# A two-layer hybrid decoder trunk on one core: indexer scores by row halves, unnormalised differential softmaxes, longer booking of chained VectorE steps, and padded products

## The chip, the cores and the metric

The kernel runs on one core of a Trainium2 chip. The metric is the device time of one execution in microseconds (us), as a median over runs. Below, PE is the matrix engine (TensorE), PEld its loading of weights, DVE the VectorE, ACT the ScalarE, POOL the GpSimd, SP the engine that issues most DMAs.

## What is computed

Two layers over 256 tokens of width 1024, in float32. Each layer has a mixer of three attention groups (A, B, C) and a gated MLP, each followed by a layer norm:

```
h = LN(ALPHA*h + mixer(h));  h = LN(ALPHA*h + conv_gated_mlp(h))
A: s = q.k*scale + cum[q] - cum[k], causal;            o_a = softmax(s) v
B: score = sum_i w_i * relu(qi_i . ki) over 8 heads of 64, causal
   sel   = top 64 keys by score;                       o_b = softmax(q.k over sel) v
C: p0, p1 = two softmaxes of q.k over 64 columns each, causal
   o_c = rms_norm((p0 - lam*p1) v, g) * (1 - lam_init)
mixer = (g_a*(o_a W_a) + g_b*(o_b W_b) + g_c*(o_c W_c)) W_out
```

## The kernel before

**Weights.** All large products are made of two float32r halves: a weight tile of 128 x 512 is split into a high half (ACT copies it rounded) and a low half (DVE subtracts it from the raw tile); both stand in one tile `hl` (16 buffers, `HL_BUFS`). A product of activations and weights is then three matmuls, high-high, low-high, high-low (`mm3`, L397; `unit_x`, L652; `unit_w`, L679). One `hl` tile of 512 columns serves both blocks of 128 tokens, so it feeds six matmuls. Weights stream from HBM by SP in the order of use (`Stream`, L112).

**The order of the work.** The program is written out by Python generators. The main line emits the big projections; attention groups are side tasks that are advanced by `tick()` after each group of three matmuls. Where a task's next step is emitted is decided by a planner, `Clocks` (L196): it books an estimated cost for each instruction on its engine (`cost`, L205; `note`, L230), and `ready` (L387) holds a task back until the planner's clock says that its inputs are done. `refill` (L177) emits the next weight split by the same clocks. The engines themselves run their instructions in the order in which they were emitted. Every operation is issued in a wrapper (`Engine`, L259), so that all of them carry L267 in the profile, and the tile names tell them apart.

**The parts that the change touches**, once per layer each:
- `task_g1` (L722) makes, among other things, `augL` (16 x 256) and `augR` (16 x 4 x 256) on DVE: the cumulative forget gates of A as operands with 16 rows. `task_A` (L992) multiplies them into each of its three score banks, between the mask (`m`, `negid`, bf16) and the products of q and k.
- `task_index` (L859) computes the indexer: 8 heads of 64 rows, of which even heads lie in rows 0 to 63 of the operands and odd ones in rows 64 to 127. `jobs` are (query block, heads) in pairs, even heads and then odd ones, run by `par` side by side. Each job is one bank of scores, a relu on ACT, and a chain of DVE steps `s = rl * w + s`. Eight rounds of max and match-replace follow for the top 64, and then `sel`.
- `soften` (L900) is a softmax: negated row maximum (DVE), exponentials with row sums (ACT), reciprocal (DVE), and, with `norm`, a multiplication by it (DVE).
- `task_C` (L1006) makes two softmaxes, `a` (normalised) and `p` (not), combines them on DVE as `a = p * rinv + a`, where `rinv` holds -lam over the sum, transposes `a` on PE, multiplies by the values, and applies an RMS norm: squares on ACT with sums `ssq`, a power on POOL (`rr`), and a scaled copy on DVE (`oc`).

Rotary embedding (`rope`, L694) of the indexer's and of C's queries and keys is four DVE steps, after which PE transposes them (`task_rope_T`, L835). Banks of PSUM are taken by `att` (one) and `att2` (two at once).

Of the kernel before, what the change touches and what calls it, by code (L numbers as in the profile page):

```python
# [10 lines left out]
F32 = mybir.dt.float32  # L11
R32 = mybir.dt.float32r
# [183 lines left out]
class Clocks:  # L196
# [3 lines left out]
    def __init__(self):  # L200
        self.clk = dict(PE=0.0, DVE=0.0, ACT=0.0, POOL=0.0)
        self.done, self.by, self.read = {}, {}, {}
        self.table = "exp"

    def cost(self, eng, op, out, args):  # L205
        n = math.prod(out.shape[1:])
# [23 lines left out]
    def note(self, eng, op, args, kw):  # L230
        aps = [x for x in list(args) + list(kw.values()) if isinstance(x, bass.AP)]
        if op == "preload_act_table_set":
            self.clk[eng] += 1280
            self.table = "exp"
        if not aps:
            return
        out = aps[0]
        outs = [part(out)] + ([kw["accum_out"].name] if "accum_out" in kw else [])
        if op == "dma_start":
            self.done[out.name] = max(self.clk[eng], self.clk["PE"]) + 4000  # L240
            return
        start = max([self.clk[eng]] + [self.done.get(n, 0) for n in map(part, aps[1:]) if self.by.get(n) != eng])
        self.clk[eng] = start + self.cost(eng, op, out, aps)
        if "accum_out" in kw:
            self.clk[eng] += 155
        if eng == "ACT" and len(args) > 2 and args[2] in TABLES and TABLES[args[2]] != self.table:
            self.table = TABLES[args[2]]
            self.clk[eng] += 1280
        for o in outs:
            self.done[o] = self.clk[eng] + (150 if eng == "PE" else 230)  # L250
            self.by[o] = eng
        for x in aps[1:]:
            self.read[x.name] = self.clk[eng]
# [62 lines left out]
def tile_hybrid(ctx: ExitStack, tc: tile.TileContext, a: dict, out: bass.AP):  # L316
# [55 lines left out]
    def t4(shape, dt=F32, n="t4"):  # L372
        return s4.tile(shape, dt, name=nm(n), tag="s4")
# [7 lines left out]
    def t1(shape, n, dt=F32):  # L381
        return s1.tile(shape, dt, name=nm(n), tag="s1")
# [326 lines left out]
    def layer(l, hT, hflag):  # L709
# [12 lines left out]
        def task_g1(g1):  # L722
# [69 lines left out]
            chr_ = t1([16, 256], "chr", R32)  # L792
            cl = t1([16, 256], "cl")
            t_ = t1([16, 256], "ct")
            augL = t1([16, 256], "augL", R32)
            augR = t4([16, 4, 256], R32, "augR")
            col = lambda i: cst[0:16, C_COL + i:C_COL + i + 1]
            ve.tensor_copy(chr_, c16)
            ve.tensor_copy(ch, chr_.bitcast(F32))
# [5 lines left out]
            ve.scalar_tensor_tensor(ch, cl, col(5), ch, ALU.mult, ALU.add)  # L805
            for q in range(4):
                ve.tensor_scalar(augR[:, q, :], ch, cst[0:16, C_BM + q:C_BM + q + 1], None, ALU.mult)
            F["aug"] = (augL, augR)

            yield from ready("PE", kvT, wul)  # L810
            bk = yield from att()
# [47 lines left out]
        def task_index():  # L859
            yield from need("qiT", "kiT", "biw")  # L860
            qiT, kiT, biw = F["qiT"], F["kiT"], F["biw"]
            s0 = t2([P, P], n="s0")
            s1 = t2([P, 256], n="s1")
            sx = [s0, s1]

            jobs = [(0, [0, 2, 4, 6]), (0, [1, 3, 5, 7]), (1, [0, 2]), (1, [1, 3]), (1, [4, 6]), (1, [5, 7])]

            def job(qb, hs):
                kw = P * (qb + 1)
                bk = yield from att()  # L870
                for n, i in enumerate(hs):
                    o = 64 * (i % 2)
                    mm(bk[:, n * kw:(n + 1) * kw], qiT[o:o + 64, i // 2, qb * P:(qb + 1) * P],
                       kiT[o:o + 64, 0:kw], n == 0)
                yield from ready("ACT", bk)
                rl = t2([P, len(hs), kw])
                sc.activation(rl, bk.rearrange("p (n k) -> p n k", n=len(hs)), AF.Relu)
                att_free(bk)
                for n, i in enumerate(hs):
                    prev = (m38[:, 256 - kw:256] if i == 0 else sx[qb])  # L880
                    ve.scalar_tensor_tensor(sx[qb], rl[:, n, :], biw[:, qb, i:i + 1], prev, ALU.mult, ALU.add)

            for i in range(0, 6, 2):
                yield from par(job(*jobs[i]), job(*jobs[i + 1]))
            mx = small([P, 2, 8], "mx")
            for r in range(TOPK // 8):
                yield from ready("DVE", s0, s1)
                for qb in (0, 1):
                    ve.max(mx[:, qb, :], sx[qb])
                for qb in (0, 1):  # L890
                    ve.match_replace(sx[qb], mx[:, qb, :], sx[qb], PICKED)
                yield
            sb0 = cpool.tile([P, P], BF16, name=nm("sb0"), tag="sb0")
            sb1 = cpool.tile([P, 256], BF16, name=nm("sb1"), tag="sb1")
            ve.scalar_tensor_tensor(sb0, s0, PICK_T, m01[:, P:256], ALU.is_gt, ALU.add)
            ve.scalar_tensor_tensor(sb1, s1, PICK_T, m01, ALU.is_gt, ALU.add)
            F["sel"] = (sb0, sb1)


        def soften(bk, ms, pt, rinv, norm=True):  # L900

            yield from ready("DVE", bk)
            v = bk.rearrange("p (n k) -> p n k", n=len(ms))
            mx = small([P, 4], "smx")
            ve.tensor_reduce(mx[:, :len(ms)], v, AX.X, ALU.max, negate=True)
            sm = small([P, 4], "ssm")
            for n, m in enumerate(ms):
                sc.activation(pt[:, m, :], v[:, n, :], AF.Exp, bias=mx[:, n:n + 1],
                              accum_out=sm[:, n:n + 1])
# [96 lines left out]
        def task_C():  # L1006
# [2 lines left out]
            a0, p0 = t2([P, 4, P], n="a0"), t2([P, 4, P], n="p0")  # L1009
            a1, p1 = t4([P, 4, 256], n="a1"), t4([P, 4, 256], n="p1")  # L1010
            rina = small([P, 2, 4], "rina")
            rinv = small([P, 2, 4], "rinv")

            def scores(qb, ms):
# [5 lines left out]
                for n, m in enumerate(ms):  # L1020
                    for c in range(2):
                        mm(bks[c][:, n * kw:(n + 1) * kw],
                           qcT[64 * c:64 * c + 64, m, qb * P:(qb + 1) * P],
                           kcT[64 * c:64 * c + 64, m, 0:kw], False)
                yield from par(soften(bks[0], ms, (a0, a1)[qb], rina[:, qb, :]),
                               soften(bks[1], ms, (p0, p1)[qb], rinv[:, qb, :], norm=False))
            yield from par(scores(0, [0, 1, 2, 3]), scores(1, [0, 1]), scores(1, [2, 3]))
            ve.tensor_scalar(rinv, rinv, nlam[:, l:l + 1], None, ALU.mult)
            for qb, (pp, aa) in enumerate(((p0, a0), (p1, a1))):
                for m in range(4):  # L1030
                    ve.scalar_tensor_tensor(aa[:, m, :], pp[:, m, :], rinv[:, qb, m:m + 1], aa[:, m, :],
                                            ALU.mult, ALU.add)
            yield from ready("PE", a0, a1)
            q0 = t4([P, 4, 256], n="q0")
            q1 = t2([P, 4, P], n="q1")
# [6 lines left out]
            def job(qb):  # L1042
# [6 lines left out]
                yield from ready("ACT", bk)  # L1049
                for m in range(4):  # L1050
                    sc.activation(oc[:, qb, m * P:(m + 1) * P], bk[:, m * P:(m + 1) * P], AF.Square,
                                  accum_out=ssq[:, qb, m:m + 1])
                ve.tensor_scalar(ssq[:, qb, :], ssq[:, qb, :], 1.0 / P, RMS_EPS, ALU.mult, ALU.add)
                gp.tensor_tensor(rr[:, qb, :], ssq[:, qb, :], mhalf[:, :4], ALU.pow)
                yield from ready("DVE", rr)
                for m in range(4):
                    ve.scalar_tensor_tensor(oc[:, qb, m * P:(m + 1) * P], bk[:, m * P:(m + 1) * P],
                                            rr[:, qb, m:m + 1], dg[:, l, :], ALU.mult, ALU.mult)
# [340 lines left out]
```

## Time and profile before

| | |
|---|---|
| median of 3 runs | 927.51 us (927.25 to 927.71) |
| the profiled execution | 927.42 us |
| its span, first to last instruction | 925.6 us |
| PE busy | 903.9 us, 98% |
| DVE busy | 658.6 us, 71% |
| ACT busy | 510.4 us, 55% |
| POOL busy | 46.4 us, 5% |
| mean share of the granted PE clock | 0.996 |

Shares of busy time are averages over the span. In the timeline, each line gives the start, the duration of the run of equal instructions, and in brackets the idle time before it with what ended it. Matmuls overlap in the record: what one costs is the distance from its start to the next start. A float32 matmul stands as two.

### The profile page before, as it was taken

The numbers are of one execution on the slowest core, as the hardware profiler recorded it, in microseconds if no ns is written. First come the engines' busy times: TensorE is split into PE (matmuls) and PEld (weight loads), VectorE is DVE, ScalarE is ACT, GpSimd is POOL, SyncE is SP. The second block draws the span as 40 slices with busy tenths as digits, with TensorE's granted clock in tenths as the row PEclk, the third lists the DMA queues.
The fourth block names the chain that finished last, engine by engine and source line by source line (L and its number), as shares of the span: only waits on it lengthen the run. The fifth ranks groups of instructions, "written<-read, shape, count | busy, mean of one in ns | idle before, by whom it ended". The sixth has DMA issues, their size and how long they took to land. (4 is left out here: it accounts for less than half of the span.)

```text
span 925.6 us, 14457 instructions
## 1 busy us (share of the span) xinstructions
PE 903.9 (98%) x5329; PEld 787.8 (85%) x5329; DVE 658.6 (71%) x1283; ACT 510.4 (55%) x1006; POOL 46.4 (5%) x63
## 2 busy tenths in 40 slices
PE   7999999999999999999999999999999999999996
PEld 4877887888888999999988788888888799999995
DVE  7788677766678766766787956667667886766755
ACT  4754765655537655655455455665555375655540
POOL 6100000011000000000000000000110100000000
PEclk9999999999999999999999999999999999999999
DMA  8823356556636665565444323548675385566501
GB/s 289 303 91 114 95 171 231 193 199 221 204 122 225 215 200 187 180 200 182 131 157 152 113 91 114 188 138 286 187 245 172 119 277 186 177 192 186 180 18 46
DMA packets 46681, 161.47 MB, mean 174 GB/s; under 512 B 5841, under 2 KB 6865, under 8 KB 46609
## 3 DMA queue, kind: packets, MB, share of 16 engines
q1 hardware_dynamic: 44208, 155.20, 51.1%
q0 software_dynamic: 1408, 4.98, 1.7%
q8 instruction: 42, 0.69, 0.3%
q10 hardware_dynamic: 992, 0.35, 0.1%
q14 instruction: 31, 0.25, 0.1%
HBM read 159.47 MB, written 1.05 MB: 173 GB/s over the span
## 5 line engine op out<-in xcount | busy, mean ns | idle before, releaser
L267 DVE TENSOR_TENSOR hl<-raw,hl 128x512 fp32r<-128x512 f32 (+1 forms) x578 | 387.3, 696 | 186.6 <-ACT hl L267 184.7
L267 ACT ACTIVATE hl<-raw 128x512 fp32r<-128x512 f32 (+1 forms) x584 | 347.4, 625 | 192.9 <-PE att L267 94.1
L267 PE MATMUL acc<-hl,hTh 128*128 128x512 f32 (+1 forms) x896 | 276.8, 390 | 2.5 <-ACT hTh L267 2.1
L267 PE MATMUL att<-hTh,hl 128*128 128x256 f32 x1280 | 231.5, 283 | 0.0
L267 PEld LDWEIGHTS att<-hTh,hl 128*128 128x128 f32 x1280 | 200.8, 192 | 1.4
L267 PEld LDWEIGHTS acc<-hl,hTh 128*128 128x128 f32 x896 | 166.9, 188 | 37.7 <-ACT hTh L267 3.7
L267 PE MATMUL att<-hTl,hl 128*128 128x256 f32 x640 | 181.1, 283 | 0.0
L267 PE MATMUL acc<-hl,hTl 128*128 128x512 f32 (+1 forms) x448 | 165.5, 387 | 0.9 <-DVE hTl L267 0.9
L267 PE MATMUL acc<-hl,act 128*128 128x512 f32 x528 | 123.4, 390 | 0.0
L267 PEld LDWEIGHTS att<-hTl,hl 128*128 128x128 f32 x640 | 122.8, 192 | 0.0
L267 PEld LDWEIGHTS acc<-hl,act 128*128 128x128 f32 x528 | 97.9, 188 | 19.5
L267 PEld LDWEIGHTS acc<-hl,hTl 128*128 128x128 f32 x448 | 84.5, 189 | 17.7 <-DVE hTl L267 2.4
L267 PE MATMUL acc<-hl,oT 128*128 128x512 f32 x288 | 68.3, 391 | 0.0
L267 PEld LDWEIGHTS acc<-hl,oT 128*128 128x128 f32 x288 | 53.7, 188 | 10.9
L267 DVE SCALAR_TENSOR_TENSOR cv<-att,convp,cv 128x255 f32<-128x255 f32 x88 | 40.4, 480 | 16.1 <-ACT cv L267 14.5
L267 PE MATMUL acc<-hTh,hl 128*128 128x256 f32 x256 | 48.7, 289 | 3.0 <-DVE hl L267 2.6
L267 PE MATMUL acc<-hl,mT 128*128 128x512 f32 x192 | 45.4, 392 | 0.0
L267 PEld LDWEIGHTS acc<-hTh,hl 128*128 128x128 f32 x256 | 39.9, 191 | 5.5 <-DVE hl L267 3.2
L267 PEld LDWEIGHTS acc<-hl,mT 128*128 128x128 f32 x192 | 35.6, 188 | 7.1
L267 ACT ACTIVATE hTh<-att 128x512 fp32r<-128x512 f32 x16 | 9.6, 597 | 49.1 <-PE att L267 43.1
L267 PE MATMUL acc<-hTl,hl 128*128 128x256 f32 x128 | 36.2, 283 | 0.0
L267 ACT ACTIVATE t<-att 128x512 f32<-128x512 f32 (+1 forms) x32 | 18.2, 599 | 28.3 <-PE att L267 23.1
(162 smaller groups left out, 686.6 us busy)
## 6 DMA issues: line engine op xcount, KB each, us to landing
raw<-in_w_dram SPq DMA_DIRECT2D x284, 512.0 KB, 4.3
raw<-in_w_dram SPq DMA_DIRECT2D x8, 332.0 KB, 3.8
lng<-in_ln_g_dram POOLq DMA_DIRECT2D x4, 512.0 KB, 4.2
lnb<-in_ln_b_dram POOLq DMA_DIRECT2D x4, 512.0 KB, 5.5
h<-in_x_dram SPq DMA_DIRECT2D x4, 256.0 KB, 4.7
lng<-in_ln_in_g_dram SPq DMA_DIRECT2D x1, 512.0 KB, 8.1
lnb<-in_ln_in_b_dram SPq DMA_DIRECT2D x1, 512.0 KB, 10.2
wu<-in_w_ukv_dram POOLq DMA_DIRECT2D x2, 256.0 KB, 5.8
```

The costliest lines, as they stand in the source:

```text
L267: f(*args, **kw)
```

## The change

It has six parts. (1) The indexer's scores are emitted by one job for each of three (query block, heads) groups; it takes two banks at once and alternates matmuls of an even head (rows 0 to 63) with the next odd head's (rows 64 to 127). The groups run one after another. (2) `augL` and `augR` get 128 partitions, which POOL sets to zero; the sixteen rows are written as before, and A multiplies all 128. (3) C's first softmax is no longer normalised: the row sums `suma` are kept, `rinv` becomes -lam * suma / sum(p), so that `a` carries a factor `suma`, which `rina` takes out again at the squares (a scale on ACT) and in `rr` (one more small DVE step for each query block). (4) The combining steps are emitted in pairs, with a yield after each. (5) The planner books 110 ns more for a DVE instruction that reads what the DVE instruction before it wrote. (6) By that, most of the mixer's order comes out differently.

```diff
-        self.table = "exp"
+        self.table, self.prev = "exp", ""
...
         start = max([self.clk[eng]] + [...])
+        if eng == "DVE" and self.prev in map(part, aps[1:]):
+            start += 110
         self.clk[eng] = start + self.cost(eng, op, out, aps)
+        if eng == "DVE":
+            self.prev = part(out)
...
-            augL = t1([16, 256], "augL", R32)
-            augR = t4([16, 4, 256], R32, "augR")
+            augL_ = t1([P, 256], "augL", R32)
+            augR_ = t4([P, 4, 256], R32, "augR")
+            gp.memset(augL_.bitcast(F32), 0.0)
+            gp.memset(augR_.bitcast(F32), 0.0)
+            augL, augR = augL_[0:16], augR_[0:16]
...
-            F["aug"] = (augL, augR)
+            F["aug"] = (augL_, augR_)
...
-            jobs = [(0, [0, 2, 4, 6]), (0, [1, 3, 5, 7]), (1, [0, 2]), (1, [1, 3]), (1, [4, 6]), (1, [5, 7])]
             def job(qb, hs):
                 kw = P * (qb + 1)
-                bk = yield from att()
+                bks = yield from att2()
                 for n, i in enumerate(hs):
-                    o = 64 * (i % 2)
-                    mm(bk[:, n * kw:(n + 1) * kw], qiT[o:o + 64, i // 2, qb * P:(qb + 1) * P],
-                       kiT[o:o + 64, 0:kw], n == 0)
-                yield from ready("ACT", bk)
...
+                    for c in range(2):
+                        o = 64 * c
+                        mm(bks[c][:, n * kw:(n + 1) * kw], qiT[o:o + 64, i // 2, qb * P:(qb + 1) * P],
+                           kiT[o:o + 64, 0:kw], n == 0)
+                for c, bk in enumerate(bks):
+                    yield from ready("ACT", bk)
...
+                    yield
...
-            for i in range(0, 6, 2):
-                yield from par(job(*jobs[i]), job(*jobs[i + 1]))
+            for qb, hs in ((0, [0, 2, 4, 6]), (1, [0, 2]), (1, [4, 6])):
+                yield from job(qb, hs)
...
-            sm = small([P, 4], "ssm")
+            sm = small([P, 4], "ssm") if sums is None else sums[:, ms[0]:]
...
-                yield from par(soften(bks[0], ms, (a0, a1)[qb], rina[:, qb, :]),
-                               soften(bks[1], ms, (p0, p1)[qb], rinv[:, qb, :], norm=False))
+                yield from par(soften(bks[0], ms, (a0, a1)[qb], rina[:, qb, :], False, suma[:, qb, :]),
+                               soften(bks[1], ms, (p0, p1)[qb], rinv[:, qb, :], False))
...
-            ve.tensor_scalar(rinv, rinv, nlam[:, l:l + 1], None, ALU.mult)
+            ve.scalar_tensor_tensor(rinv, rinv, nlam[:, l:l + 1], suma, ALU.mult, ALU.mult)
             for qb, (pp, aa) in enumerate(((p0, a0), (p1, a1))):
                 for m in range(4):
+                    if m % 2 == 0:
+                        yield from ready("DVE", pp)
                     ve.scalar_tensor_tensor(aa[:, m, :], pp[:, m, :], rinv[:, qb, m:m + 1], aa[:, m, :],
                                             ALU.mult, ALU.add)
+                    if m % 2:
+                        yield
...
                     sc.activation(oc[:, qb, m * P:(m + 1) * P], bk[:, m * P:(m + 1) * P], AF.Square,
-                                  accum_out=ssq[:, qb, m:m + 1])
+                                  scale=rina[:, qb, m:m + 1], accum_out=ssq[:, qb, m:m + 1])
...
                 yield from ready("DVE", rr)
+                ve.tensor_tensor(rr[:, qb, :], rr[:, qb, :], rina[:, qb, :], ALU.mult)
```

The order of the instructions moves in three places of which the prediction speaks. In the rows, a name's last number tells instances apart.

**PE, layer 0, where C's queries are transposed** (`ident` with the tile `t_89`; `hl` are weights, `sb` is `sel`, `kbT` and `t_22` the keys and queries of B). Before:

```order
L267 MATMUL acc_848<-hl_777,hTh_162 128x512
L267 MATMUL acc_848<-hl_777,hTl_163 128x512
L267 MATMUL acc_848<-hl_777,hTh_162 128x512
L267 MATMUL att_876<-ident,t_89_845 128x128 x4
L267 MATMUL att_881<-ident,t_89_845 128x128 x4
L267 MATMUL acc_849<-hl_777,hTh_162 128x512
```

In the changed order:

```order
L271 LDWEIGHTS negid
L271 MATMUL att_1035<-sb_95_991,negid 128x512
L271 MATMUL att_1035<-kbT_739,t_22_440 128x128 x4
L271 LDWEIGHTS negid
L271 MATMUL att_1041<-sb_96_992,negid 128x512
L271 MATMUL att_1041<-kbT_739,t_22_440 128x256 x2
L271 LDWEIGHTS negid
L271 MATMUL att_1045<-sb_96_992,negid 128x512
L271 MATMUL att_1045<-kbT_739,t_22_440 128x256 x2
L271 MATMUL att_1050<-ident,t_89_830 128x128 x4
L271 MATMUL acc_939<-hl_995,hTh_162 128x512
```

The transposes stood some 33 projection matmuls after the indexer's last scores; now they stand behind 102 of them and behind B's three banks of scores.

**DVE, layer 0, where C's two softmaxes are combined** (`a`, `p` and `rinv` as above, `hl` the low halves of weights, `q` and `oT` evacuations). Before:

```order
L267 TENSOR_TENSOR hl_1336<-raw_975,hl_1336 128x512
L267 RECIPROCAL rinv_1140<-ssm_1252 128x2
L267 TENSOR_SCALAR rinv_1140<-rinv_1140,nlam 128x8
L267 SCALAR_TENSOR_TENSOR a_122_1135<-p_123_1136,rinv_1140,a_122_1135 128x128 x4
L267 SCALAR_TENSOR_TENSOR a_124_1137<-p_125_1138,rinv_1140,a_124_1137 128x256 x4
L267 TENSOR_TENSOR hl_1363<-raw_1024,hl_1363 128x512
```

In the changed order:

```order
L271 RECIPROCAL rinv_1184<-ssm_1273 128x2
L271 SCALAR_TENSOR_TENSOR rinv_1184<-rinv_1184,nlam,suma_1183 128x8
L271 SCALAR_TENSOR_TENSOR a_122_1178<-p_123_1179,rinv_1184,a_122_1178 128x128 x2
L271 TENSOR_TENSOR hl_1415<-raw_1018,hl_1415 128x512
L271 COPY q_147_1398<-att_1405 128x4x128
L271 SCALAR_TENSOR_TENSOR a_122_1178<-p_123_1179,rinv_1184,a_122_1178 128x128 x2
L271 TENSOR_TENSOR hl_1437<-raw_1104,hl_1437 128x512
L271 SCALAR_TENSOR_TENSOR a_124_1180<-p_125_1181,rinv_1184,a_124_1180 128x256 x2
L271 TENSOR_TENSOR hl_1465<-raw_1104,hl_1465 128x512
L271 TENSOR_TENSOR oT_1454<-att_1455,oT_1454 128x512
L271 TENSOR_TENSOR oT_1454<-att_1460,oT_1454 128x512
L271 SCALAR_TENSOR_TENSOR a_124_1180<-p_125_1181,rinv_1184,a_124_1180 128x256 x2
```

The eight combining steps stood in one piece, with the splits of weights behind them; now a split follows every two or so. The multiplications of `a` by `rina` (four groups before this place) are gone.

**DVE, at the start of the program, between the first norm's two scalings and its second block's transposed values** (`h_92`, `h_93` the scaled rows, `att` banks with their transposes, `gb` gain and bias). Before:

```order
L267 TENSOR_SCALAR h_93<-h_93,mv_220,rs_223 128x512
L267 TENSOR_TENSOR hl_284<-raw_116,hl_284 128x332
L267 TENSOR_TENSOR hl_291<-raw_116,hl_291 128x332
L267 TENSOR_TENSOR att_297<-att_297,gb 128x512 x2
L267 TENSOR_TENSOR att_304<-att_304,gb 128x512 x2
L267 TENSOR_TENSOR hTl_163<-att_297,hTh_162 128x4x128
```

In the changed order:

```order
L271 TENSOR_SCALAR h_93<-h_93,mv_220,rs_223 128x512
L271 TENSOR_TENSOR hl_284<-raw_116,hl_284 128x332
L271 TENSOR_TENSOR hl_291<-raw_116,hl_291 128x332
L271 TENSOR_TENSOR hl_297<-raw_119,hl_297 128x332
L271 TENSOR_TENSOR att_301<-att_301,gb 128x512 x2
L271 TENSOR_TENSOR att_308<-att_308,gb 128x512 x2
L271 TENSOR_TENSOR hTl_163<-att_301,hTh_162 128x4x128
```

A third split of 332 columns, which stood behind the low halves `hTl`, now stands ahead of the four steps on the banks.

POOL has four more instructions: two memsets in each layer (128 x 256 and 128 x 1024), behind the second load of `lamq` in layer 0 and behind the power for `rr` of the latent's norm in layer 1, and ahead of C's powers. The queue of SP is unchanged.

## Rows read from the trace of the kernel before

**Rows 1.** The page's part 1: busy us, share of the span, instructions.
```profile
PE 903.9 (98%) x5329; PEld 787.8 (85%) x5329; DVE 658.6 (71%) x1283; ACT 510.4 (55%) x1006; POOL 46.4 (5%) x63
```

**Rows 2.** Waits of PE: tile waited for, us in total, times, longest.
```profile
PE att L267 <- DVE t L267: 3.4, 2, 1.8
PE acc L267 <- DVE hl L267: 2.6, 3, 1.4
...
PE acc L267 <- ACT hl L267: 0.5, 1, 0.5
```

**Rows 3.** Timeline of PE, three places: start, us, instruction, count, idle before.
```profile
20.74 1.78 PE L267 MATMUL acc<-hl,hTh 128*128 128x512 f32 x4 [1.44 <-ACT hTh L267]
...
72.11 0.74 PE L267 MATMUL att<-ident,t 128*128 128x128 f32 x5 [1.80 <-DVE t L267]
...
120.93 0.39 PE L267 MATMUL acc<-hTh,hl 128*128 128x256 f32 x1 [1.40 <-DVE hl L267]
```

**Rows 4.** Timeline of DVE, layer 0: indexer, first rounds, C's queries, combining steps.
```profile
59.21 2.74 DVE L267 SCALAR_TENSOR_TENSOR s<-t,biw,s 128x128 f32<-128x128 f32 x7
...
65.10 2.11 DVE L267 SCALAR_TENSOR_TENSOR s<-t,biw,s 128x256 f32<-128x256 f32 x4
...
69.51 0.61 DVE L267 MAX8 mx<-s 128x8 f32<-128x128 f32 x2
...
70.68 0.42 DVE L267 TENSOR_TENSOR ru<-t,cc 128x256 f32<-128x256 f32 x1
...
117.55 2.72 DVE L267 SCALAR_TENSOR_TENSOR a<-p,rinv,a 128x128 f32<-128x128 f32 x8
120.19 1.89 DVE L267 TENSOR_TENSOR hl<-raw,hl 128x512 fp32r<-128x512 f32 x3
```

**Rows 5.** Timeline of PE, layer 0, scores of A.
```profile
146.66 0.39 PE L267 MATMUL att<-m,negid 128*128 128x512 bf16 x1
146.98 0.50 PE L267 MATMUL att<-augR,augL 16*128 16x512 f32 x1
147.41 1.16 PE L267 MATMUL att<-t,t 128*128 128x128 f32 x8
148.41 0.27 PE L267 MATMUL att<-m,negid 128*128 128x256 bf16 x1
148.61 0.50 PE L267 MATMUL att<-augR,augL 16*128 16x512 f32 x1
149.03 1.13 PE L267 MATMUL att<-t,t 128*128 128x256 f32 x4
```

**Rows 6.** Timeline of PE, layer 0, scores of B behind a projection.
```profile
83.69 0.39 PE L267 MATMUL acc<-hl,hTh 128*128 128x512 f32 x1
83.92 0.39 PE L267 MATMUL att<-sb,negid 128*128 128x512 bf16 x1
84.15 1.05 PE L267 MATMUL att<-kbT,t 128*128 128x128 f32 x8
85.04 0.38 PE L267 MATMUL att<-sb,negid 128*128 128x512 bf16 x1
```

**Rows 7.** Timeline of PE, layer 0: the indexer's first scores and C's first scores.
```profile
56.94 1.71 PE L267 MATMUL att<-kiT,t 64*128 64x128 f32 x16
...
97.56 1.16 PE L267 MATMUL att<-t,t 64*128 64x128 f32 x16
```

**Rows 8.** The same view: the indexer's second scores, then C's.
```profile
59.48 1.14 PE L267 MATMUL att<-kiT,t 64*128 64x256 f32 x8
...
98.98 1.13 PE L267 MATMUL att<-t,t 64*128 64x256 f32 x8
```

**Rows 9.** Timeline of DVE at the start of the program.
```profile
17.75 0.90 DVE L267 TENSOR_TENSOR hl<-raw,hl 128x332 fp32r<-128x332 f32 x2
```

**Rows 10.** POOL's instructions by group: count, busy us, mean ns, idle before.
```profile
L267 POOL TENSOR_TENSOR mrg<-mrg,gs 128x1024 f32<-128x1024 f32 x4 | 11.0, 2752 | 171.5 <-DVE gs L267 171.5
```

**Rows 11.** Timeline of ACT, layer 0, one relu of the indexer.
```profile
62.07 0.60 ACT L267 ACTIVATE t<-att 128x512 f32<-128x512 f32 x1 [0.78 <-DVE s L267]
```

More of the change, by code (lines that the diff above doesn't have):

```diff
@@ L864, in task_index @@
             sx = [s0, s1]
-            jobs = [(0, [0, 2, 4, 6]), (0, [1, 3, 5, 7]), (1, [0, 2]), (1, [1, 3]), (1, [4, 6]), (1, [5, 7])]
             def job(qb, hs):
                 kw = P * (qb + 1)
-                bk = yield from att()
+                bks = yield from att2()
                 for n, i in enumerate(hs):
-                    o = 64 * (i % 2)
-                    mm(bk[:, n * kw:(n + 1) * kw], qiT[o:o + 64, i // 2, qb * P:(qb + 1) * P],
-                       kiT[o:o + 64, 0:kw], n == 0)
-                yield from ready("ACT", bk)
[L876 to L881, printed above, removed]
-            for i in range(0, 6, 2):
-                yield from par(job(*jobs[i]), job(*jobs[i + 1]))
+                    for c in range(2):
[4 more added lines that the diff above has]
+                    yield from ready("ACT", bk)
+                    rl = t2([P, len(hs), kw])
+                    sc.activation(rl, bk.rearrange("p (n k) -> p n k", n=len(hs)), AF.Relu)
+                    att_free(bk)
+                    for n, i in enumerate(hs):
+                        prev = (m38[:, 256 - kw:256] if i + c == 0 else sx[qb])
+                        ve.scalar_tensor_tensor(sx[qb], rl[:, n, :], biw[:, qb, i + c:i + c + 1], prev,
+                                                ALU.mult, ALU.add)
+                    yield
+            for qb, hs in ((0, [0, 2, 4, 6]), (1, [0, 2]), (1, [4, 6])):
+                yield from job(qb, hs)
             mx = small([P, 2, 8], "mx")
@@ L897, in task_index, with soften @@
             F["sel"] = (sb0, sb1)
-        def soften(bk, ms, pt, rinv, norm=True):
+        def soften(bk, ms, pt, rinv, norm=True, sums=None):
             yield from ready("DVE", bk)
@@ L1011, in task_C @@
             rina = small([P, 2, 4], "rina")
+            suma = small([P, 2, 4], "suma")
             rinv = small([P, 2, 4], "rinv")
```

## The prediction

> **What bounds the kernel now.** I read the busy shares first: PE is busy for 98% of the span, DVE for 71%, ACT for 55% [rows 1]. So the time is the length of PE's list plus the pauses in it, and DVE or ACT count only where PE stops for them. The waits of PE come next [rows 2]. Of those that this change can reach, two, 3.4 us in all, are transposes that wait for a rotated tile of DVE; three, 2.6 us, are projections that wait for a low half of weights from DVE, and one, 0.5 us, for a high half from ACT. The timeline gives them their places [rows 3]: C's query transposes at 72.11 after 1.80 us (the twin in layer 1 has the other 1.6), a projection at 120.93 after 1.40, and the first product of the program at 20.74 after 1.44 for `hTh`. Last, what DVE does before each of them [rows 4]. Before 72.11 it runs the indexer's chained steps `s` (seven in 2.74 us, 0.39 each; four wide ones in 2.11, 0.53 each), one top-k round (69.51 to 70.68, 1.17 us) and the rotation. `cost` books a step at 110 + 1.2 ns a column, 264 and 417 ns. Eight steps of each are 8 x 0.125 + 8 x 0.11 = 1.9 us more than booked: about the wait. Before 120.93 it runs eight combining steps without a break, 117.55 to 120.19, and the split that PE needs stands behind them.
>
> The sum is made against the profiled execution, 927.42 us, 0.1 under the median; about 1.8 us of it lie outside its span of 925.6.
>
> **The waits, -6.5 us.** With 110 ns more per chained step, the planner books 374 and 527 ns, what the rows show. It now puts C's query transposes behind 102 projection matmuls and B's banks. On DVE, the rotation stands behind the last round, `sel` and three splits. It is done near 89.0 (the sum is below) and PE is there near 90.2: the two waits for `t` go, -3.4. The eight combining steps are parted, a split behind each two, so a split waits for two steps (0.7 us) instead of eight (2.6), and DVE loses the four multiplications by `rina` ahead of them: -2.6. I also count the 0.5 of ACT's high half as gone, as it stands next to the same places. The low end of this term is nothing at all; see the first rival.
>
> **Padded products, -2.3 us.** In A's first bank the mask's product takes 0.32 to the next start, the one of 16 rows 0.43, and the products of q and k 1.00: 1.75 us [rows 5]. B's bank is the same but for the 16 rows and shows the price when every product has 128: 0.23 for a mask product behind a 128-row one, 0.89 for the eight [rows 6]. The 16-row product is 256 columns in two records, and with 128 rows I take it at 0.23, as a projection of 512 columns [rows 6]. That makes 0.23 + 0.23 + 0.89 = 1.35, a gain of 0.40. A wide bank now has 0.20 for the mask and 0.42 for the 16 rows [rows 5]; I take 0.12 (half the columns of the 0.23) and 0.23, and 0.11 off the first product behind, as above: 0.38. Per layer 0.40 + 2 x 0.38 = 1.16. Bounds: nothing, if a product of 16 rows costs its 0.43 for another reason; not more than the 0.43 + 0.32 - 0.23 = 0.52 of the first bank three times over, 3.1 in two layers.
>
> The Trainium skill ("TensorE: Matmul & The Clock Gate", "Why this matters for your kernels") says that a single matmul with 32 rows takes the same time as one with 128, rows being saved by running tiles beside each other only. By it alone this term would be 0 and the time 920.5; that is the third rival. The skill's page "TensorEngine Tiling (Array Packing)" (on changing the tiling mode) has PE drained at the change, which the 0.32 and 0.43 beside 0.23 agree with, and which the padding avoids.
>
> The zeroing is on POOL, which is idle here. Four memsets: the nearest row, a product of 128 x 1024, is 2752 ns [rows 10], which I take as the upper end; the lower is next to nothing. They are issued before the sixteen rows are computed, so DVE's writes to `augL` and `augR` wait only if POOL comes late. I take 0; at worst, where a whole 2.75 us is in the way, DVE is some 1.5 us late in each layer at a place where PE has splits in store, +1 in all.
>
> **Alternating the indexer's halves, -1.1 us.** The first scores of query block 0 run for 1.71 us, sixteen records of one half after the other's; C's, of the same shape and already alternating, for 1.16 [rows 7]: -0.55 in each layer. The wide scores take 1.14 already, as C's alternating ones do (1.13) [rows 8]: nothing there.
>
> **The start, +0.4 us.** A third split of 332 columns stands ahead of DVE's four steps on the banks; two take 0.90 us [rows 9], one 0.4. The next wait there is PE's for `hTh` [rows 3], which comes from those banks, so 1.44 becomes about 1.85. Nothing hides it: PE has nothing else to do there. Lower bound 0 if the split's data come late enough that ACT sets the chain; upper 0.45.
>
> **The top-k of layer 0, +0.3 us.** The projections that were spread around C's transposes now run in one stretch that DVE must feed while it does the top-k. PE: first scores from 56.94, now done at 58.1; six matmuls, 1.5 (three took 0.83 between the first scores and the wide ones [rows 7, 8], and three more at 0.23); wide scores 1.1; six matmuls, 1.5; wide scores 1.1: at 63.4 the stretch begins, and 102 x 0.23 = 23.5 us later, at 86.9, come B's masks. DVE: first step at 59.21 - 0.55 = 58.7, then 16 steps (8 x 0.39 + 8 x 0.53 = 7.3), seven rounds before the last split (8.2), and 15 splits at 1.89 / 3 = 0.63 (9.5) [rows 4]. Split by split, in the order of the program, I set DVE's end beside PE's first use: the third comes at 67.9 and is used at 68.2, the fourth 69.7 and 69.6, the fifth (behind the second round) 71.5 and 71.0, the seventh 73.9 and 73.7, the last 83.7 and 84.8. So PE is short of a tile by up to 0.5 us in the first rounds, and not later. I take 0.3. Nothing is the lower bound; a DVE that begins 1.5 us later than I have it would make 2. Behind it the last round (1.17), `sel` (0.9, as one step `s` of each width), three splits (1.9) and the rotation (three times the 0.42 of its first step) end near 89.0; PE, after three banks of B at 85.04 - 83.92 = 1.12 [rows 6], is there at 90.2. In layer 1 the rotation still stands behind the first round and I find it 0.5 us ahead of PE: 0.
>
> **At nothing:** the scale on ACT's squares (an operand, no instruction); the two small steps on `rr`, each behind POOL's power and ahead of `oc`, for which PE has projections and the next group of scores; the `suma` factor (it replaces a step). If that cover were gone, two small steps in each layer, at most as long as a step of 128 columns (0.39), are 1.6. The queue of SP is unchanged.
>
> **Sum:** 927.42 - 6.5 - 2.3 - 1.1 + 0.4 + 0.3 = 918.2 us.
>
> **Rivals.**
> *The waits move instead of going.* DVE does nearly the same work, and where a stall of PE goes, PE asks for the next split earlier; a place after B's scores or behind the combining steps may be late next. For it: the top-k stretch has margins of 0.3 us and less, and POOL's and ACT's shares of C's chain are unchanged. Against it: DVE is idle for 29% of the span and sixteen tiles of `hl` can stand ready. Half of the 6.5 back gives 921.5, all of it 924.7. Chance 0.22.
> *Lock step of ACT and DVE in the indexer, slower.* A relu of ACT waits for DVE's steps on the tile whose place it takes; this is in the trace of before: 0.78 us ahead of a relu of 0.60 [rows 11]. The new job emits both relus of a pair in a row, with high halves behind them on ACT, and DVE's low halves wait for these. If relu and split followed each other strictly, each of the twelve relus of the program would cost PE, whose stretch has no cover, 0.60 + 0.63 = 1.23 us: 14.8 us, 933.0. It decides from the ninth of twelve on (9 x 1.23 = 11.1, over the gain of 9.2 and the 1.9 to be seen). Against it: even now that relu waits 0.78, and PE's list of waits has none for it. Chance 0.05.
> *Padding gives nothing:* what the skill's rule above says of a single product; by the rows, that the 0.43 belongs to the data type or to the shape of the output. 918.2 + 2.3 = 920.5. Against it the 0.32 ahead of the 16-row product, which a cost of its own can't explain. Chance 0.08.
> *All waits back and no gain of the padding:* 927.0, chance 0.03.
>
> **How the numbers follow.** The forecast has 0.62. The range runs from 916.0 (a padding of 3.1, no price at the start or in the top-k, 916.7, and 0.7 for smaller waits) to 923.0 (half of the waits back, and 1.5 from the memsets or DVE's late start). It leaves out the lock step, the combined case and the waits that come back whole, together a little under 2 in 10. A measurement of this kernel tells 0.2%, 1.9 us, from no change: faster is below 925.6, slower above 929.4. Faster are the forecast, the padding rival and most of the first: 0.90; the same 0.05; slower, the lock step, 0.05.
>
> **What will show it.** In the profile after: no line for DVE's `t` among PE's waits, and `hl` at 0.5 us or less; a start-to-start distance of 0.23 behind the padded product, and no longer first product of q and k; 1.1 us for the indexer's first scores; the wait at the first product near 1.85; waits of up to 0.5 in the 102 matmuls; POOL's memsets done before DVE writes `augL`. I am wrong if PE's waits on DVE add up to over 3 us again, if they reappear inside the top-k stretch, or if ACT's relus there wait longer than the 0.78 of before and PE with them.

## The result, and the profile after

| | before | changed |
|---|---|---|
| median | 927.61 us (4 runs, 927.25 to 927.90) | 917.07 us (4 runs, 916.76 to 917.12) |
| span of the profiled execution | 925.6 us | 915.0 us |
| ratio | | 0.9885, 95% interval 0.9871 to 0.9899 |

The forecast was 918.2 us in a range of 916.0 to 923.0, with 0.90 on faster. The time came out 1.1 us under it. How much of that is right for the reasons given is what the rest is about: some of the steps were wrong, and their errors partly cancel.

The page's part 1 of the changed kernel, to be set beside [rows 1]. PE's share is the same 98%; its busy time fell by 4.3 us, and the rest of the 10.6 us was idle time.

```profile
PE 899.6 (98%) x5329; PEld 787.5 (86%) x5329; DVE 654.2 (71%) x1271; ACT 510.7 (56%) x1006; POOL 49.3 (5%) x67
```

All waits of PE in the changed kernel (tile waited for, us in total, times, longest):

```profile
PE acc L271 <- ACT hTh L271: 4.0, 8, 2.1
PE att L271 <- DVE spin L271: 1.1, 1, 1.1
PE att L271 <- DVE h L271: 0.8, 1, 0.8
PE acc L271 <- DVE hl L271: 0.3, 1, 0.3
PE acc L271 <- POOL hl L271: 0.3, 1, 0.3
PE acc L271 <- ACT hl L271: 0.3, 1, 0.3
```

Against [rows 2], the line of DVE's `t` (3.4 us) is gone, `hl` of DVE fell from 2.6 to 0.3, and ACT's from 0.5 to 0.3. New is that `hTh` of ACT stands at 4.0 us with eight waits, where it was 2.1 with two. (The line of DVE's `h`, 0.8 us here, is at the start; it varies from one execution to the next, with 2.2 us for the same order in the kernel with 16 rows below.)

The timeline of PE in the changed kernel, at the start, the indexer, B's scores, behind C's first scores, A's scores, and a layer norm (start, us, instruction, count, idle before):

```profile
21.16 2.08 PE L271 MATMUL acc<-hl,hTh 128*128 128x512 f32 x4 [2.08 <-ACT hTh L271]
...
57.53 1.16 PE L271 MATMUL att<-kiT,t 64*128 64x128 f32 x16
...
87.25 0.39 PE L271 MATMUL att<-sb,negid 128*128 128x512 bf16 x1
...
90.52 0.60 PE L271 MATMUL att<-ident,t 128*128 128x128 f32 x4
...
110.93 0.39 PE L271 MATMUL acc<-hTh,hl 128*128 128x256 f32 x1 [0.28 <-ACT hl L271]
111.66 0.38 PE L271 MATMUL acc<-hTh,hl 128*128 128x256 f32 x1 [0.34 <-DVE hl L271]
...
143.53 0.39 PE L271 MATMUL att<-m,negid 128*128 128x512 bf16 x1
143.57 0.58 PE L271 MATMUL att<-augR,augL 128*128 128x512 f32 x1
143.99 1.05 PE L271 MATMUL att<-t,t 128*128 128x128 f32 x8
144.88 0.27 PE L271 MATMUL att<-m,negid 128*128 128x256 bf16 x1
...
272.06 1.20 PE L271 MATMUL acc<-hl,hTh 128*128 128x512 f32 x4 [0.25 <-ACT hTh L271]
```

- The indexer's first scores take 1.16 us, as C's did, instead of 1.71 [rows 7].
- A's narrow bank, from mask to mask, takes 144.88 - 143.53 = 1.35 us instead of 1.75 [rows 5], as forecast. Mask and product together take 143.99 - 143.53 = 0.46, the 0.23 + 0.23 of the sum (the record parts them as 0.04 and 0.42, so neither can be read by itself), and the products of q and k 0.89 instead of 1.00.
- B's masks come at 87.25 (forecast 86.9) and C's query transposes at 90.52 (90.2), without a wait. In the stretch of 102 matmuls ahead of them no wait is recorded.
- The first product waits 2.08 us for `hTh`, where 1.85 was forecast. It starts 0.42 us later than before (21.16 against 20.74 [rows 3]).

Both kernels run the same 4656 projection matmuls in the same order, so the start of the n-th one in both traces shows where the 10.6 us came from (a table of mine from the two traces; differences are taken before rounding):

| place | before | changed | difference | since the place above |
|---|---|---|---|---|
| start, projection 160 | 53.90 | 53.82 | -0.09 | -0.09 |
| end of A in layer 0, 560 | 157.52 | 152.52 | -5.00 | -4.91 |
| behind the first norm of layer 0, 1120 | 292.54 | 287.66 | -4.88 | +0.12 |
| behind the norm between the layers, 2400 | 482.82 | 478.32 | -4.50 | +0.38 |
| end of A in layer 1, 2880 | 606.97 | 596.20 | -10.78 | -6.28 |
| behind the first norm of layer 1, 3440 | 742.38 | 731.72 | -10.66 | +0.12 |
| near the end, 4640 | 913.45 | 902.79 | -10.65 | +0.01 |

So the two mixers gave 11.2 us, three norms took 0.6 back, and the start shows no difference between these two executions.

POOL's memsets in layer 0, which the sum had at nothing, took 0.33 and 0.97 us and were done over 8 us ahead of DVE's first write to `augL`, at 49.37 (in layer 1 over 8 us as well):

```profile
39.70 0.33 POOL L271 MEMSET augL<- 128x256 f32 x1
39.95 0.97 POOL L271 MEMSET augR<- 128x1024 f32 x1
```

### The profile page after: what moved, and what is told of

It is laid out like the page before. It is cut to its first block, busy times and chain, and to the rows that moved or that the text cites. A ratio compares the mean times of both kernels' runs of the same rounds, so it can differ in the third digit from the quotient of the medians.

```text
span 915.0 us, 14449 instructions
## 1 busy us (share of the span) xinstructions
PE 899.6 (98%) x5329; PEld 787.5 (86%) x5329; DVE 654.2 (71%) x1271; ACT 510.7 (56%) x1006; POOL 49.3 (5%) x67
## 5 line engine op out<-in xcount | busy, mean ns | idle before, releaser
L271 POOL TENSOR_TENSOR rs<-mv,mhalf 128x1 f32<-128x1 f32 x10 | 9.5, 949 | 484.1 <-DVE mv L271 484.1
```

The costliest lines, as they stand in the source:

```text
L271: f(*args, **kw)
```

## The parts one by one

Which part removes which wait? The prediction gave the two waits for `t` to the longer booking and those for `hl` to the softmax. Four kernels each add one part to the kernel before. In the first, only the planner's lines are added:

```diff
+        if eng == "DVE" and self.prev in map(part, aps[1:]):
+            start += 110
...
+        if eng == "DVE":
+            self.prev = part(out)
```

> The kernel before with the longer booking alone. In its order C's query transposes stand behind 33 projection matmuls after the indexer's last scores in both layers (33 and 42 before), not behind 102. Theory of the prediction, that the booking cures the two waits for DVE's t: both gone, 3.4 us, and the layer norms' transposes in one piece cost 0.7: about 924.8 us. Rival, that the new form of the indexer's job moved the transposes: the waits for t stay above 1 us each in this kernel, and only the 0.7 of the norms is added: 927.5 to 928.3 us.

Measured: 923.34 us, ratio 0.9949 (0.9934 to 0.9964), faster by 4.4. Both waits for `t` are gone, though the transposes still stand 33 matmuls behind the indexer. DVE's timeline shows how (first top-k round, rotation, second round):

```profile
69.80 0.61 DVE L271 MAX8 mx<-s 128x8 f32<-128x128 f32 x2
...
70.97 0.42 DVE L271 TENSOR_TENSOR ru<-t,cc 128x256 f32<-128x256 f32 x1
...
72.17 0.61 DVE L271 MAX8 mx<-s 128x8 f32<-128x128 f32 x2
```

The rotation now stands behind the first round. In the kernel before it stands behind the second [rows 4]; the first is this one:

```profile
67.73 0.62 DVE L267 MAX8 mx<-s 128x8 f32<-128x128 f32 x2
```

The rotation is done near 72.2, and PE starts the transposes at 72.40, with hardly a pause (1.80 us before [rows 3]). In layer 1 the rotation moves from behind the third round to behind the first. The booking cured the wait by moving DVE's work, and not by moving PE's transposes. The longest wait for `hl` also fell, from 1.40 to 0.56 us.

The second kernel has the indexer's new job alone:

```diff
-                bk = yield from att()
+                bks = yield from att2()
...
+                    for c in range(2):
+                        o = 64 * c
+                        mm(bks[c][:, n * kw:(n + 1) * kw], qiT[o:o + 64, i // 2, qb * P:(qb + 1) * P],
+                           kiT[o:o + 64, 0:kw], n == 0)
...
+            for qb, hs in ((0, [0, 2, 4, 6]), (1, [0, 2]), (1, [4, 6])):
+                yield from job(qb, hs)
```

> The kernel before with the indexer's new job alone (both halves from two banks, alternating). Its order already has C's query transposes of layer 0 behind 93 projection matmuls and B's banks. Theory of the prediction: 1.1 us from the alternation and no more, 926.4 us. Rival, that the job's form moves the transposes: both waits for t go too, 3.4 us with 0.3 of slow matmuls behind them: 922.7 us. The wait for hl behind the combining steps (1.40 in layer 0) stays under both.

Measured: 922.40 us, ratio 0.9939 (0.9923 to 0.9956), 5.4 faster: the rival's number, not that of the prediction's theory. The waits for `t` are gone here as well, and the one for `hl` stays:

```profile
PE acc L267 <- DVE hl L267: 3.1, 2, 1.7
```

In layer 0 it is this part that puts the transposes behind some hundred projections and B's banks (93 here, 102 in the whole change). I put that down to the job's form (one job holds two banks, and `par` no longer runs two of them side by side); no run takes this apart. In layer 1 the transposes do not come later: they stand behind 36 projections, and stood behind 42. There the wait goes because DVE's rotation moves, from behind the third top-k round to behind the second, with two splits of weights between DVE's first step and it instead of five. DVE in layer 1 of the kernel before (the third round, the rotation):

```profile
521.66 0.62 DVE L267 MAX8 mx<-s 128x8 f32<-128x128 f32 x2
...
522.84 0.42 DVE L267 TENSOR_TENSOR ru<-t,cc 128x256 f32<-128x256 f32 x1
```

and of this kernel (the second round, the rotation), with PE's transposes, which do not wait:

```profile
516.78 0.61 DVE L267 MAX8 mx<-s 128x8 f32<-128x128 f32 x2
...
517.96 0.41 DVE L267 TENSOR_TENSOR ru<-t,cc 128x256 f32<-128x256 f32 x1
...
519.91 1.03 PE L267 MATMUL att<-ident,t 128*128 128x128 f32 x8
```

Third, the unnormalised softmax with the combining steps in pairs, alone:

```diff
-                               soften(bks[1], ms, (p0, p1)[qb], rinv[:, qb, :], norm=False))
+                               soften(bks[1], ms, (p0, p1)[qb], rinv[:, qb, :], False))
...
+                    if m % 2:
+                        yield
```

> The kernel before with the unnormalised first softmax and the combining steps in pairs alone. Theory: the waits for hl near the combining steps fall from 2.6 to under 0.6 and the two waits for t stay at 1.8 and 1.6: about 925.0 us. Rival, that DVE is late for the next split anyway: a wait of over 1 us comes back within 10 us of the steps, 927.0 us or more.

Measured: 924.86 us, ratio 0.9970 (0.9958 to 0.9981), 2.9 faster. The waits of PE moved as the theory said:

```profile
PE att L267 <- DVE t L267: 3.4, 2, 1.8
...
PE acc L267 <- ACT hl L267: 0.6, 1, 0.6
...
PE acc L267 <- DVE hl L267: 0.3, 1, 0.3
```

The two long waits for `hl` are gone, 2.2 us; the third, of 0.3, and the one for ACT's high half (0.5 before [rows 2]) stay. Whether the pairs do it or the multiplications that fall away is not shown, as no kernel has one without the other.

Fourth, the padded products alone:

```diff
-            augL = t1([16, 256], "augL", R32)
+            augL_ = t1([P, 256], "augL", R32)
...
-            F["aug"] = (augL, augR)
+            F["aug"] = (augL_, augR_)
```

> The kernel before with augL and augR of 128 rows alone; the order on PE and DVE is that of before. Theory: 0.40 for the narrow bank and 0.38 for each wide one, in two layers 2.3 to 2.6 us: 925.0 us, with PE's waits as before. Rival, that rows of a single product don't matter: 927.5 us.

Measured: 925.58 us (ten runs, 925.29 to 927.34), ratio 0.9980 (0.9971 to 0.9989), 2.2 faster. The table of places gives -1.19 and -1.18 us at A of the two layers, as the sum had it (-1.16 each).

The four gains, by medians, come to 14.8 us (4.41 + 5.35 + 2.89 + 2.17); the whole change gives 10.5. The waits for `t`, 3.4 us, are counted twice in the sum, since either of two parts removes them.

## The parts taken out again

The next three kernels are the whole change less one part; their edits undo the diffs above. First the planner's lines:

> The changed kernel without the longer booking. The indexer's new job alone keeps C's transposes behind 93 projections and B's banks in layer 0. Theory, that either of the two cures the waits for t and the booking now only costs at the norms: no wait for t, 916.4 us. Rival, that the booking is still needed in layer 1 or in the stretch of the top-k: a wait of 1 us or more there, 918 us or more.

Measured: 916.13 us, ratio 0.9879 (0.9864 to 0.9893). No wait for a rotated tile is left in the mixers, and the norms' new waits for `hTh` are gone: the theory. Against the waits for `t` the booking does nothing here that the indexer's job has not done, and it costs the norms. What it costs in all is not clear of noise: 0.9 us by the medians, 0.6 by the ratios to the kernel before, with intervals that overlap. By the projections, the norms give back 0.6 us against the changed kernel; A's end in layer 0 comes 0.7 earlier than there, where the two waits at 110.93 and 111.66 are gone as well; and layer 1's mixer takes 0.8 longer, with no wait recorded in it. One wait shows at the start, 1.34 us for `t`; the section on the start explains it.

Then the indexer's job:

> The changed kernel with the indexer's old job (one bank each, halves one after the other). C's transposes stand behind 33 projections again in both layers. Theory, that the longer booking alone is enough against the waits for t (it puts the rotation one top-k round earlier): waits for t of 0.1 us at most, the indexer's first scores 1.64 us again, 918.2 us. Rival, that in the whole change the new job is what removes them: waits for t of 1 us or more come back, 920 us or more.

Measured: 918.34 us, ratio 0.9898 (0.9883 to 0.9913). The two waits for `t` are 0.04 and 0.06 us. This is the theory's number: with the booking there, the new job is worth 1.3 us by the medians, with intervals that overlap. That this is near the alternation's 1.1 is in part chance. Alternating gives 0.55 in each layer, but by the projections A of layer 0 ends at 152.52 in both kernels, and the whole difference lies in layer 1 (597.79 against 596.20). In layer 0 the kernel without the new job lacks the two waits at 110.93 and 111.66, which makes up for its slower scores.

And the softmax part:

> The changed kernel with the first softmax normalised and the eight combining steps of C in one piece. Theory, that the block of steps makes the next split late: a wait for hl of 1 to 1.7 us behind it in each layer, about 919.9 us. Rival, that the other parts already moved the splits ahead so that nothing waits: 917.1 us.

Measured: 918.39 us, ratio 0.9895 (0.9880 to 0.9909), its runs from 916.48 to 918.87. The theory failed:

```profile
PE acc L271 <- DVE hl L271: 0.6, 2, 0.3
```

Eight combining steps in one piece make no wait over 0.35 us here. I put that down to the order of the splits, which the other parts move; no run takes it apart. In layer 0 the two waits at 110.93 and 111.66 are there with and without the part; there DVE itself had waited for ACT's high halves. So the part removes 2.2 us of waits where it comes alone, and one of 0.2, in layer 1, where the other parts are there. By the projections its lack costs nothing in layer 0's mixer and 0.5 us in layer 1's. The 1.3 us between the medians are not clear of noise: the intervals overlap, and 0.6 us of the difference between the two profiled executions lies at the start, where both kernels have the same order.

## What the rows of a product cost

Two kernels use the whole change and multiply 16 or 64 of the 128 rows only. The edit, for 64:

```diff
-                mm(bk.rearrange("p (n k) -> p n k", n=len(ms)), augL[:, qb * P:(qb + 1) * P],
-                   augR[:, ms[0]:ms[0] + len(ms), 0:kw], False)
+                mm(bk.rearrange("p (n k) -> p n k", n=len(ms)), augL[0:64, qb * P:(qb + 1) * P],
+                   augR[0:64, ms[0]:ms[0] + len(ms), 0:kw], False)
```

> The changed kernel, but A multiplies only the sixteen rows of augL and augR that carry values; the order of all instructions is that of the changed kernel and POOL still zeroes. Theory, that a product of fewer rows than its neighbours makes PE drain before and after it: 0.40 and 2 x 0.38 per layer come back with the wider masks' part, 2.5 us in all: 919.6 us. Rival, that padding is worth nothing here and the gain of the padded kernel alone came from elsewhere: 917.1 us.

> The changed kernel with 64 rows of augL and augR in the product; order unchanged. Drain at a change of the number of rows: 64 rows differ from the neighbours' 128 as 16 do, so the time is that of 16 rows, 919.6 us, with 0.3 to 0.4 from the mask's start to the product's. Rival, that the cost grows with the rows that are missing: 917.9 to 918.5 us.

Measured: 919.17 us with 16 rows (ratio 0.9911, 0.9896 to 0.9926) and 919.50 with 64 (0.9915, 0.9900 to 0.9930). The timeline with 64 rows:

```profile
143.56 0.39 PE L271 MATMUL att<-m,negid 128*128 128x512 bf16 x1
143.88 0.50 PE L271 MATMUL att<-augR,augL 64*128 64x512 f32 x1
144.30 1.16 PE L271 MATMUL att<-t,t 128*128 128x128 f32 x8
145.30 0.27 PE L271 MATMUL att<-m,negid 128*128 128x256 bf16 x1
```

Mask, product, scores and next mask start 0.32, 0.42 and 1.00 us apart, as with 16 rows [rows 5]: 1.74 us against 1.35 with 128. Between 16 and 64 rows it does not matter how many are missing, only that the number differs from the neighbours'. By the projections, A gives up 1.1 to 1.2 us in each layer in both kernels. This settles the rival on padding. The page "TensorEngine Tiling (Array Packing)" of the Trainium skill has PE drained when the tiling mode changes (Tiling Modes). These rows agree with it, 0.32 and 0.42 us where neighbours alike take 0.23, if a product of fewer rows counts as another mode; the drain itself no run shows. The page "TensorE: Matmul & The Clock Gate" of the Trainium skill (Why this matters for your kernels) says that a single matmul of 32 rows takes as long as one of 128. No run here times one by itself; among products of 128 rows, fewer rows cost 0.4 us a bank.

## The norms and the start

In the whole change the booking touches every chained DVE instruction, those of the norms too. One kernel keeps it for the chained steps of the form that the indexer and C use:

```diff
-        if eng == "DVE" and self.prev in map(part, aps[1:]):
+        if eng == "DVE" and op == "scalar_tensor_tensor" and self.prev in map(part, aps[1:]):
```

> The changed kernel, the 110 ns booked only for chained scalar_tensor_tensor steps and not for every chained DVE instruction. Its order has the layer norms' transposes in two pieces again with three matmuls between, and two splits of 332 columns ahead of the bank steps at the start. Theory, that the longer booking of the norms' short chains cost 0.7 us at the four norms, and nothing net at the start: 916.4 us, PE's waits for hTh down from 4.0 to about 2. Rival, that the norms' price is set by something else: 917.1 us or more.

Measured: 917.40 us, ratio 0.9891 (0.9875 to 0.9908). The norms are as before again and give back 0.6 us by the projections, but in the mixers the other order costs more than that, +0.4 in layer 0 and +0.8 in layer 1. The start has the order of the kernel before and a wait for `t` of 1.35 us. The theory had the mechanism and missed the sum: the planner's clock is one, and what is booked less at one place moves splits at others.

At the start, the table shows no loss although the wait for `hTh` grew by 0.65 us. PE next stops for the first rotated tile, and DVE has that between 31.5 and 32.0 in all these kernels. In the kernel without the booking:

```profile
31.68 1.06 PE L267 MATMUL att<-ident,t 128*128 128x128 f32 x8 [1.34 <-DVE t L267]
```

PE's clock fits in here. The windows of the kernel before (us, busy us and count of PE, PEld, DVE, ACT and POOL, share of the granted clock, DMA share, GB/s):

```profile
21.00:24.50 3.50, 3.50 (x10) 2.64 (x10) 3.31 (x7) 3.06 (x6) 2.59 (x8) 0.51 0.92 210
```

and of the one without the booking:

```profile
21.00:24.50 3.50, 3.47 (x15) 2.55 (x14) 3.26 (x7) 3.13 (x6) 2.53 (x8) 1.00 1.05 202
```

One ran at the lower level (1.2 GHz) behind the wait for `hTh` and was at the transposes at 31.75, with hardly a wait; the other ran at 2.4 GHz, came early, and waited 1.34 us until 31.68. Six kernels, these two among them, have the same order at the start. In three the granted clock was 1.00 in that stretch, and PE waited 1.34 to 1.35 us for `t`; in the other three it was 0.51 to 0.55, and PE waited 0.04 to 0.05. Projection 80 starts at 33.82 to 34.31 in the first three and at 33.88 to 34.27 in the others: the rotated tile sets the time, not the clock. The six kernels with the changed kernel's start have projection 80 at 33.79 to 34.36, and once at 35.27, where the granted clock was still 0.60 from 24.50 to 28.00. So the later first product costs next to nothing as a rule, and once it went with 1.4 us.

The last kernel tries to use this: the masks' three steps on DVE are made earlier, by one number in the kernel without the booking.

```diff
-        for _ in range(24):
+        for _ in range(8):
             yield
         masks()
```

> The changed kernel without the longer booking, and with the three small mask steps of DVE at the start (0.6 us) put where DVE was idle at 24 to 27 us, ahead of four splits; C's and the keys' first transposes stand six matmuls later by that. Theory, that the start is decided by DVE's first rotation (PE waited 1.34 us for it where its clock had not dropped): that wait gone and 0.5 to 1.0 us gained, 915.1 to 915.6 us. Rival, that the loads or PE's own list decide the start: 916.1 us.

Measured: 915.66 us (915.18 to 916.48), ratio 0.9870 (0.9854 to 0.9889), the lowest median here, 1.4 us under the changed kernel and 0.5 under the one without the booking; the intervals overlap with both, so runs alone do not tell them apart. All waits of PE in it:

```profile
PE acc L267 <- ACT hTh L267: 1.4, 1, 1.4
PE att L267 <- DVE h L267: 1.4, 2, 0.8
PE att L267 <- DVE spin L267: 1.1, 1, 1.1
PE acc L267 <- DVE hTl L267: 0.9, 2, 0.5
```

The wait for `t` is gone, and projection 80 comes 0.48 us earlier than without the move. The reason is not the one I gave: DVE still starts the rotation at 30.33, since the split ahead of it waits for ACT; what helped is that the transposes stand six matmuls later in PE's list and PE has work until then. Counted from the end of the rotation, projection 80 starts 1.73 us later here, and 2.25 to 2.28 in the six executions above. But this execution ran at the lower level behind the wait for `hTh`:

```profile
21.00:24.50 3.50, 3.50 (x11) 2.73 (x10) 2.77 (x8) 3.29 (x7) 2.87 (x9) 0.57 0.93 174
```

Whether six matmuls cover the wait at 2.4 GHz too, no run shows.

## Why the prediction was right, and where it was not

**The waits, -6.5 us.** PE's waits for `t` and `hl` in the mixers fell from 6.4 to 0.6 us, 5.8. Of the distance from one start to the next more goes: at 72.11 it was 2.19 us, the wait's 1.80 and the 0.39 of the matmul ahead, of which only 0.23 is its cost when the next one follows. Each wait removed so gives another 0.16, four fewer of them 0.6. Together 6.4: the size was right. The step's cause was half wrong, in the sentence "it now puts C's query transposes behind 102 projection matmuls and B's banks": the indexer's new job does that, as the kernel with it alone shows, and in layer 0 only. The booking moves the rotation, by one top-k round in layer 0 and two in layer 1, where the new job moves it by one. Either part is enough in both layers. The reading of DVE ahead of 72.11 also had a round too few: two ran there, from 67.73 and from 69.51.

**The combining steps, inside that term,** are given to the pairs and the missing multiplications. (These are eight in each layer, in three groups, and not four: DVE has 12 instructions less in all, 16 multiplications less and four small steps more.) Alone this part removes 2.2 of the 2.6 us, and ACT's 0.5 stays. In the whole change all of these are gone, and two waits of 0.28 and 0.34 us are new in layer 0, as in all kernels here with both the booking and the new job, and in no other: that much of the first rival came true. The kernel without the part puts it at 0.5 us there by the projections, and at 1.3 by medians that are not clear of noise: the other parts move the splits as well.

**Padding, -2.3.** Right in size and cause: -2.2 alone by medians, 2.1 taken out again, 2.4 by the places. The term calls the 16-row product 256 columns in two records; it is one record of 512 columns [rows 5], and the price of 0.23, that of a projection of 512 columns, stands.

**Alternation, -1.1.** The 32 records of the first scores took 1.09 us less in all, the wide ones the same. That this edit would also reorder the whole stretch was not in its term, though the order rows ahead of the prediction show the new order.

**The start, +0.4,** failed at "Nothing hides it: PE has nothing else to do there". The first product did start 0.42 us later, and projection 160 came at the same time (-0.09). PE stops next for DVE's first rotated tile; whoever comes late there waits less.

**The top-k, +0.3,** did not come: no wait is recorded in the 102 matmuls. The tightest margin was worked out at -0.5 us from a split of 0.63 us, and PE reached B's masks 0.35 us later than reckoned; both are within the sum's error.

**The norms, which had no term,** cost 0.6 us. The prediction says nothing of them. In the changed kernel both blocks' transposes stand in one piece, and PE then waits 0.25 to 0.30 us for `hTh` twice at each norm. In exchange the wait for `hTl`, 0.47 us at the first norm of each layer before, is gone; so the norm between the layers, which had none, lost most.

**What is left:** the terms give 6.4 + 2.4 + 1.1 = 9.9 us in the mixers, the places 11.2. Of the other 1.3 us, some 0.6 are three short pauses of the kernel before (0.03, 0.08 and 0.09 us, too short for the list of waits) with the 0.16 or less that each adds as above. The last 0.7 lie in distances between matmuls without a pause; I have not taken them apart. The 1.3 us and the two costs that did not come (0.4 and 0.3) outweigh the norms' 0.6. They make the 1.4 us by which the profiled execution (916.76) is under the forecast; by the median it is 1.1.

The lock step of ACT and DVE did not show: the indexer's relus paused up to 1.55 us on ACT (0.89 before), but PE recorded no wait there. Of moved waits, the two in layer 0 are all.

## What to carry to other kernels

When a change has several parts and a planner reorders everything, ask of each part alone what order it gives before a gain is put down to it: here two parts each remove the same 3.4 us, and the kernel that has only one of them, the new job, is no slower than the one with both. A small product whose number of rows differs from its neighbours' should be padded to theirs if the zeros are free: the difference cost 0.4 us each time here, whether 16 or 64 rows were used. Before a later start is priced, look for the next place where PE stops anyway.

## What the runs showed that was not expected

A wait of PE may cost more than its length. The profiled execution of the padded kernel took 927.34 us; eight of its ten runs lie at 925.3 to 925.9. In it PE waited 1.91 us for `t` in layer 1, and the windows behind it show the granted clock at 0.63:

```profile
523.80:528.00 4.20, 4.20 (x17) 3.47 (x18) 4.20 (x20) 2.64 (x5) 0.00 (x0) 0.63 0.08 31
```

The same stretch of the kernel before, behind a wait of 1.57 us, kept its clock:

```profile
524.20:528.00 3.80, 3.74 (x21) 3.26 (x22) 3.80 (x16) 2.65 (x5) 0.00 (x0) 1.00 0.13 50
```

Matmuls there start 0.43 us apart instead of 0.23, and the next projections came 1.9 us later against the kernel before. These are single executions: that the wait brought the lower clock on is not shown, only that it came right behind it here and not there. A time for such a wait from one trace may be too small.
